# The embedding gates and the HGRN values as Strassen-type 2x2 block products, in a kernel for one Trainium2 core

## The chip, the core and the metric

The kernel runs on one core of a Trainium2 chip. A core has a matrix engine (TensorE, PE in the profile, with its weight loads as PEld), a vector engine (VectorE, DVE), an activation engine (ScalarE, ACT), GpSimd (POOL) and SyncE (SP), whose queue issues most of the loads; POOL issues the others. Each engine works through its own instructions in order and waits for others by semaphores. The metric is the time of one execution on the device in microseconds (us); lower is better.

## The reference, cut to what matters

512 tokens, width 1024, two layers. Layer 0 mixes tokens by multi-head latent attention, layer 1 by HGRN2, a gated linear recurrence.

```python
for i in range(2):
    h = mla_mixer(x, ...) if i == 0 else hgrn2_mixer(x, ...)
    x = layer_norm(alpha * x + h, ...)
    x = layer_norm(alpha * x + (silu(x @ w_g) * (x @ w_u)) @ ffn_w_down[i], ...)
    x = x + sigmoid(x @ ple_w_gate[i]) * (p[i] @ ple_w_proj[i])
# in hgrn2_mixer: proj = x @ w_in; q, f, v, gate are its four parts of 1024 columns
```

The change concerns three products of 512 x 1024 by 1024 x 1024: `x @ ple_w_gate[0]`, `x @ ple_w_gate[1]`, and the values `v` of the HGRN2 layer.

## The kernel before, in words

Tokens lie in four tiles of 128. Every float32 product is made of three matmuls on split operands: each operand is cut into a high part of fewer bits and a low part (the rest), and `mm3` adds high·high, high·low and low·high in PSUM. `split` makes both parts: ACT copies the source into the high part with rounding, DVE subtracts it from the source for the low part. `split_dma` does without DVE: ACT writes the high part, ACT writes its negative into the low part, and a DMA issued by POOL adds the source from memory onto that. `unit` loads a weight unit of 128 x 1024 by SP into one of 3 buffers `raw` and splits it into `whi` and `wlo` (5 buffers each).

The activations must be transposed to be left factors. A result of a stage that is needed so is put down by `defer`, and `flush` later lets PE transpose it (`to_feat`, four 128 x 128 transposes into a `tp` bank) and calls the sink that splits it. `Pair` is the plain sink: one split per half tile. `Winograd` serves the FFN's first product, `gate_up`, which already computes 2x2 block products with seven instead of eight multiplications: its sink makes the blocks A11 to A22 and four sums S1 to S4 from them, and `prep` makes the weight sums T1 to T4 for the next block while the present one is multiplied.

`rows` is the plain product: for each token tile and half of the columns 24 matmuls of 512 columns into one bank, then `consume`. `ple` runs `ple_w_proj` (8 banks of 6 matmuls), whose banks ACT copies into `pp`, and then `rows` for the gate with a sigmoid, a product and a sum per bank. In layer 0 the result goes through a `Pair` to `hgrn`, which begins with the values, again by `rows`; in layer 1 it goes out to memory, and the last bank there is cut in two of 256 columns (`cut`).

Each engine's order is fixed when the kernel is built: a scheduler places the instructions on the engines by the order of the program, the buffers' reuse and its own estimates. Buffers that matter here: 14 large slots (`big`), five buffers of 128 x 1024 under each of the tags `ma` and `mb`, and eight PSUM banks (`ps` three, `sc` two, `tp` two, `wg` one).

Of the kernel before, what the change touches and what calls it, by code (L numbers as in the profile page):

```python
# [20 lines left out]
F32 = mybir.dt.float32  # L21
F32R = mybir.dt.float32r
# [22 lines left out]
SM_SCALE = (NOPE + ROPE) ** -0.5  # L45
NLEV = 7
NEG = -1e30
T2 = 4
MID_BUFS = {"ma": 5, "mb": 5}
SLOTS = 14  # L50
# [24 lines left out]
class Rows:  # L75


    def __init__(self, b, dt=F32):
        self.z = [b.slot([P, 2, D], dt) for _ in range(NT // 2)]

    def __call__(self, t, cols=slice(None)):
        return self.z[t // 2][:, t % 2, cols]
# [14 lines left out]
        self.b.split(hi, lo, ps)  # L97


class Winograd:  # L100

    def __init__(self, b):
        self.b = b
        two = lambda: [b.slot([P, 2, 4, 256], F32R) for _ in range(2)]
        self.a1, self.s13, self.s24 = two(), two(), two()
        self.a2 = [b.slot([P, 2, 4, 256], F32R) for _ in range(2)]
        self.raw = [b.mid([P, 4, 256]) for _ in range(2)]  # L110
        self.at = {}

    def __call__(self, name):

        if name in ("A21", "A22"):
            z = self.a2[name == "A22"]
            return z[:, 0], z[:, 1]
        z, n = {"A11": (self.a1, 0), "A12": (self.a1, 1), "S1": (self.s13, 0), "S3": (self.s13, 1),
                "S2": (self.s24, 0), "S4": (self.s24, 1)}[name]
        return z[0][:, n], z[1][:, n]  # L120

    def sink(self, t, n, ps):
        b, nc = self.b, self.b.nc
        cs = slice(t % 2 * P, t % 2 * P + P)
        if t < 2:
            b.split(self.a1[0][:, n, :, cs], self.a1[1][:, n, :, cs], ps)
            nc.scalar.activation(self.raw[n][:, :, cs], ps, AF.Copy)
            return
        b.split(self.a2[n][:, 0, :, cs], self.a2[n][:, 1, :, cs], ps)
        if n == 0:  # L130
            a21 = b.small([P, 4, P], tag="t2", bufs=T2)
            nc.scalar.activation(a21, ps, AF.Copy)
            sx = b.mid([P, 2, 4, P], tag="mb")
            nc.vector.tensor_tensor(out=sx[:, 1], in0=self.raw[0][:, :, cs], in1=ps, op=ALU.subtract)
            self.at[t] = a21, sx
            return
        a21, sx = self.at.pop(t)
        sy = b.mid([P, 2, 4, P], tag="mb")
        nc.vector.tensor_tensor(out=sx[:, 0], in0=ps, in1=a21, op=ALU.add)
        nc.vector.tensor_tensor(out=sy[:, 0], in0=ps, in1=sx[:, 1], op=ALU.subtract)  # L140
        nc.vector.tensor_tensor(out=sy[:, 1], in0=self.raw[1][:, :, cs], in1=sy[:, 0], op=ALU.subtract)
        b.split(self.s13[0][:, :, :, cs], self.s13[1][:, :, :, cs], sx)
        b.split(self.s24[0][:, :, :, cs], self.s24[1][:, :, :, cs], sy)


class Builder:
# [201 lines left out]
        return self.small([P, 4], tag="lnst", bufs=6)  # L348


    def rows(self, lhs, units, consume, cut=()):

        for t in range(NT):
            n = 256 if t in cut else 512
            for c in range(0, 512, n):
# [8 lines left out]
                consume(t, slice(c, c + n), ps)  # L364

    def out_proj(self, lhs, src, x, ln):

        xT = Winograd(self)
        gb = self.ln_params(ln)
        st = [self.new_stats() for _ in range(NT)]  # L370
        self.rows(lhs, [self.unit(src[0, u]) for u in range(4)], lambda t, c, ps: self.ln_half(x, t, 0, ps, st[t]))
# [4 lines left out]
        self.rows(lhs, [self.unit(src[1, u], u % 2 == 0) for u in range(4)], fin)  # L376
        return xT


    def gate_up(self, l, xT):  # L380
# [3 lines left out]
        nc, v = self.nc, self.nc.vector  # L384
# [85 lines left out]
        for half in range(2):  # L470
            for j in range(2):
                plain(hs[j], ws[j], half)
                self.flush()
# [4 lines left out]
    def ffn(self, l, x, xT, ln):  # L478
        hT = self.gate_up(l, xT)
        gb = self.ln_params(ln, True)  # L480
        yT = Pair(self)
        acc = [(self.bank(f), self.bank(g)) for f, g in (("tp", "tp"), ("sc", "sc"), ("ps", "ps"), ("ps", "wg"))]
# [12 lines left out]
        for k in range(NF - NL):  # L495
            w, h = self.unit(self.i["ffn_w_down"][l, k]), hsplit(k)
            for t in range(NT):
                part(k, t, h, w)
        last = [(k, self.unit(self.i["ffn_w_down"][l, k]), hsplit(k)) for k in range(NF - NL, NF)]
        for t in range(NT):  # L500
            for k, w, h in last:
                part(k, t, h, w)
            self.flush()
            st = self.new_stats()
            for n in range(2):
                self.ln_half(x, t, n, acc[t][n], st)
            self.ln_finish(x, t, st, gb, yT.sink)
        return yT


    def ple(self, l, x, xT, last):
        nc = self.nc
        praw = self.mid([P, 2, S])
        nc.sync.dma_start(praw, self.i["p"][l])
        pT = (self.mid([P, 2, S], F32R), self.mid([P, 2, S], F32R))
        self.split(pT[0], pT[1], praw)
        pp = Rows(self)
        yT = None if last else Pair(self)
        for n in range(2):
            w = self.unit(self.i["ple_w_proj"][l, n])  # L520
            for t in range(NT):
                ps = self.bank()
                for k in range(2):
                    self.mm3(ps, [z[:, k, t * P:(t + 1) * P] for z in pT], [z[:, k * 512:(k + 1) * 512] for z in w], k == 0, k == 1)
                nc.scalar.activation(pp(t, slice(n * 512, (n + 1) * 512)), ps, AF.Copy)
        self.flush()
        for n in range(2):
            def fin(t, c, ps):
                sg = self.small([P, 512], tag="t2", bufs=T2)[:, c]
                c = slice(n * 512 + c.start, n * 512 + c.stop)  # L530
                nc.scalar.activation(sg, ps, AF.Sigmoid)
                xs = x(t, c)
                nc.vector.tensor_tensor(out=sg, in0=sg, in1=pp(t, c), op=ALU.mult)
                nc.vector.tensor_tensor(out=xs, in0=xs, in1=sg, op=ALU.add)
                if yT is None:
                    nc.sync.dma_start(self.out[:, t, c], xs)
                else:
                    self.defer(xs, yT.sink, t, n)
            self.rows(xT, [self.unit(self.i["ple_w_gate"][l, n, u]) for u in range(4)], fin, (NT - 1,) if last and n else ())
        return yT  # L540


# [196 lines left out]
    def hgrn(self, xT):  # L739
        nc = self.nc  # L740
        v_, a_ = nc.vector, nc.scalar
        i = self.i
# [6 lines left out]
        for n in range(2):  # L749
            def fin(t, c, ps):  # L750
                a_.activation(vv(t, slice(n * 512, (n + 1) * 512)), ps, AF.Copy)
            self.rows(xT, [self.unit(i["hgrn_w_v"][n, u]) for u in range(4)], fin)

        on = Rows(self)
        W2 = 4 * P
# [8 lines left out]
        for p in range(H // 2):  # L764
# [7 lines left out]
            for hh in range(2):  # L772
# [4 lines left out]
                for q in range(2):  # L777
                    w = self.unit(i["hgrn_w_fq"][h, q])
                    ps = self.bank()
                    for kc in range(KC):  # L780
                        self.mm3(ps, [z[:, kc * P:(kc + 1) * P] for z in w], xT(kc), kc == 0, kc == KC - 1)
# [192 lines left out]
```

## Time and profile before

| | before |
|---|---|
| median of 3 runs | 1299.7 us (1298.95 to 1300.2) |
| profiled execution | 1299.13 us, span 1297.0 us |
| PE busy | 1272.0 us (98%) |
| PE weight loads | 1134.2 us (87%) |
| DVE busy | 809.7 us (62%) |
| ACT busy | 658.5 us (51%) |
| POOL busy | 154.7 us (12%) |
| bytes read from memory | 153.05 MB |

Shares are of the span. The matmuls' busy time is modelled and overlaps, so how long a row of matmuls takes is read from their starts. "L200" is a line of the kernel; lines of helpers (L179, L180: `split`; L200 to L202: `mm3`) stand for all who call them, and the names of the tiles tell which call it is.

### The profile page before, as it was taken

To read this page: it belongs to the slowest core of one execution; us is meant where nothing else is said; L and a number is where in the kernel's file an instruction comes from. 1 tells how busy PE (TensorE), PEld (TensorE's weight loads), DVE (VectorE), ACT (ScalarE), POOL (GpSimd) and SP (SyncE) were. 2 spreads that over 40 slices of the span, in tenths; PEclk is the share of its full clock that TensorE was granted. 3 is DMA by queue.
4 is the path that set the end of the run, shared out by engine and by line. 5 is a ranking of instruction groups with operands and counts; after the bars stand their busy time and mean duration, and the time that the engine had idled before them with its cause. 6 is when DMAs were issued, how large, how long until landed. Compare 5 with 4: busy or idle time off the path is not lost.

```text
span 1297.0 us, 20093 instructions
## 1 busy us (share of the span) xinstructions
PE 1272.0 (98%) x7900; PEld 1134.2 (87%) x7900; DVE 809.7 (62%) x1452; ACT 658.5 (51%) x1140; POOL 154.7 (12%) x167
## 2 busy tenths in 40 slices
PE   8999999999999999999999999999999999999998
PEld 8788889999999888888888887888999999888887
DVE  7998488677675332943377776449777676433463
ACT  6666357767764222533334344327767765422352
POOL 0200041111110000100002220023111111000000
PEclk9999999999999999999999999999999999999999
DMA  7213027877884323232412120323888786323231
GB/s 228 68 63 131 26 89 180 210 181 175 186 187 136 98 98 114 85 109 65 133 62 66 66 78 21 115 80 86 213 205 186 181 186 164 119 97 98 94 98 49
DMA packets 47614, 156.45 MB, mean 121 GB/s; under 512 B 5664, under 2 KB 5920, under 8 KB 47264
## 3 DMA queue, kind: packets, MB, share of 16 engines
q1 hardware_dynamic: 36000, 123.71, 29.7%
q0 software_dynamic: 11520, 31.46, 14.0%
q8 instruction: 62, 1.02, 0.3%
q14 instruction: 32, 0.26, 0.1%
HBM read 153.05 MB, written 2.10 MB: 120 GB/s over the span
## 4 chain that ended last, share of the span: by engine, by line
PE 83%; DVE 7%; DMA 4%; ACT 3%; issue 2%; POOL 1%; SPq 0%; DVEq 0%; ACTq 0%; POOLq 0%
PE ps L200 18%; PE ps L201 18%; PE ps L202 18%; PE sc L200 3%; DMA raw<-ffn_w_in 3%; PE sc L201 3%; PE sc L202 3%; PE wg L201 2%; PE wg L200 2%; PE wg L202 2%; PE tp L304 2%; PE sc L812 2%; PE tp L201 2%; PE tp L202 2%; PE tp L200 2%
## 5 line engine op out<-in xcount | busy, mean ns | idle before, releaser
L180 DVE TENSOR_TENSOR wlo<-raw,whi 128x1024 fp32r<-128x1024 f32 (+1 forms) x123 | 148.4, 1209 | 206.2 <-ACT whi L179 204.5
L179 ACT ACTIVATE whi<-raw 128x1024 fp32r<-128x1024 f32 (+1 forms) x135 | 139.5, 1038 | 230.1 <-PE wg L202 125.7
L200 PE MATMUL ps<-big,whi 128*128 128x256 f32 (+1 forms) x768 | 236.9, 308 | 0.0
L202 PE MATMUL ps<-big,wlo 128*128 128x256 f32 (+1 forms) x768 | 236.7, 308 | 0.0
L201 PE MATMUL ps<-big,whi 128*128 128x256 f32 (+1 forms) x768 | 235.5, 307 | 0.0
L200 PE MATMUL ps<-whi,big 128*128 128x512 f32 (+2 forms) x440 | 170.6, 388 | 1.0 <-ACT big L179 1.0
L202 PE MATMUL ps<-whi,big 128*128 128x512 f32 (+2 forms) x440 | 168.2, 382 | 0.0
L201 PE MATMUL ps<-wlo,big 128*128 128x512 f32 (+2 forms) x440 | 168.0, 382 | 0.0
L201 PEld LDWEIGHTS ps<-big,whi 128*128 128x128 f32 x768 | 146.8, 191 | 5.4
L202 PEld LDWEIGHTS ps<-big,wlo 128*128 128x128 f32 x768 | 146.8, 191 | 5.2
L200 PEld LDWEIGHTS ps<-big,whi 128*128 128x128 f32 x768 | 146.9, 191 | 4.8
L200 PEld LDWEIGHTS ps<-whi,big 128*128 128x128 f32 x440 | 82.9, 188 | 15.4 <-ACT big L179 1.2
L202 PEld LDWEIGHTS ps<-whi,big 128*128 128x128 f32 x440 | 82.7, 188 | 15.6
L201 PEld LDWEIGHTS ps<-wlo,big 128*128 128x128 f32 x440 | 82.9, 188 | 14.4
L210 POOL TENSOR_TENSOR rr<-rv,mhalf 128x1 f32<-128x1 f32 (+2 forms) x28 | 26.6, 951 | 481.3 <-DVE rv L208 481.3
L180 DVE TENSOR_TENSOR wlo<-ma,whi 128x1024 fp32r<-128x1024 f32 x40 | 49.0, 1224 | 34.2 <-ACT whi L179 34.2
L202 PE MATMUL ps<-whi,ma 128*128 128x512 f32 x164 | 64.2, 392 | 0.0
L201 PE MATMUL ps<-wlo,ma 128*128 128x512 f32 x164 | 64.2, 392 | 0.0
L200 PE MATMUL ps<-whi,ma 128*128 128x512 f32 x164 | 64.0, 390 | 0.0
L186 POOL DMA_DIRECT2D ma<-ffn_w_in x40 | 34.8, 870 | 234.4 <-DVE big L460 150.8
L439 ACT ACTIVATE part<-ps 128x256 f32<-128x256 f32 x120 | 44.5, 374 | 25.3 <-PE ps L202 24.8
L180 DVE TENSOR_TENSOR mb<-ma,mb 128x1024 fp32r<-128x1024 f32 x40 | 48.9, 1222 | 6.3 <-ACT mb L179 3.4
(309 smaller groups left out, 3071.8 us busy)
## 6 DMA issues: line engine op xcount, KB each, us to landing
raw<-ffn_w_in SPq DMA_DIRECT2D x88, 512.0 KB, 4.6
raw<-ffn_w_down SPq DMA_DIRECT2D x44, 512.0 KB, 3.5
wlo<-ffn_w_in POOLq DMA_DIRECT2D x40, 512.0 KB, 7.3
ma<-ffn_w_in POOLq DMA_DIRECT2D x40, 256.0 KB, 7.0
raw<-ple_w_gate SPq DMA_DIRECT2D x16, 512.0 KB, 3.5
raw<-hgrn_w_fq SPq DMA_DIRECT2D x16, 512.0 KB, 3.5
raw<-mla_w_o SPq DMA_DIRECT2D x8, 512.0 KB, 3.6
raw<-hgrn_w_v SPq DMA_DIRECT2D x8, 512.0 KB, 4.4
```

Of the source, the lines that this page charges most:

```text
L179: self.nc.scalar.activation(hi, src, AF.Copy)
L180: (eng or self.nc.vector).tensor_tensor(out=lo, in0=src, in1=hi.bitcast(F32), op=ALU.subtract)
L186: self.nc.gpsimd.dma_start(lo, src, accum_op=ALU.add)
L200: mm(ps, a[0], b[0], start=start, stop=False, skip_group_check=more)
L201: mm(ps, a[0], b[1], start=False, stop=False, skip_group_check=more)
L202: mm(ps, a[1], b[0], start=False, stop=stop, skip_group_check=more)
L210: nc.gpsimd.tensor_tensor(out=r, in0=v, in1=self.mhalf[:, :n], op=ALU.pow)
L304: self.nc.tensor.transpose(out=ps[:, c * P:(c + 1) * P], in_=src[:, c * P:(c + 1) * P], identity=self.ident)
L439: copy = lambda dst, src: nc.scalar.activation(dst, src[:, :N], AF.Copy)
L812: nc.tensor.matmul(ps[:, c * P:(c + 1) * P], X[:, c * P:(c + 1) * P], pair_view(cs[0][:, :, 1, :], cs[1][:, :, 0, :]), start=True, stop=True)
```

## The change

Three pieces belong together.

First, `rows` gives way to a new function `square` for the three products. It cuts tokens (tiles 0, 1 against 2, 3), depth and columns in halves and makes seven products of 256 x 512 by 512 x 512, each 24 matmuls of 512 columns, where eight were. The weight sums T1 to T4 are made on DVE and split ("made"); three blocks are weights as they are, split by `split_dma` ("given"): SP loads each block as before, and B21 and B22 a second time for that. Partial sums are kept on ACT (128 x 512 copies) and joined with the last product by DVE in `consume`, ahead of the sigmoid.

Second, the left factors are made at the transposes for these products too: `Factors` replaces `Winograd` and, ahead of `square`, `Pair`.

Third, the token tiles go in the order 2, 3, 0, 1 in `out_proj` and `ffn`, `gate_up`'s plain units do half 1 first, `p` and its split lie in `mb` buffers, and the cut of the last bank is gone.

```diff
+ORDER = (2, 3, 0, 1)
-class Winograd:
+class Factors:
+    def __init__(self, b, whole=False, a21=True):
...
+        if whole:
+            for n in range(2):
+                w = [b.slot([P, 4, S], F32R) for _ in range(2)]
+                for m in range(2):
+                    self.z[f"A{m + 1}{n + 1}"] = [z[:, :, m * 256:(m + 1) * 256] for z in w]
+                self.z[n] = w
+            names = []
+        else:
+            names = ["A21", "A22", "A11", "A12"] if a21 else ["A22", "A11", "A12"]
+        for name in names + ["S1", "S2", "S3", "S4"]:
+            z = b.slot([P, 2, 4, 256], F32R)
+            self.z[name] = z[:, 0], z[:, 1]
...
+    def put(self, name, cs, src):
+        hi, lo = self.z[name]
+        self.b.split(hi[:, :, cs], lo[:, :, cs], src)
+
     def sink(self, t, n, ps):
+        v = self.b.nc.vector
         cs = slice(t % 2 * P, t % 2 * P + P)
+        name = f"A{2 if t >= 2 else 1}{n + 1}"
+        if name in self.z:
+            self.put(name, cs, ps)
+        if name == "A21":
+            if t == 2:
+                self.p, self.q = self.b.mid([P, 4, 256]), self.b.mid([P, 4, 256])
+            self.b.nc.scalar.activation(self.p[:, :, cs], ps, AF.Copy)
             return
+        p, q = self.p[:, :, cs], self.q[:, :, cs]
+        if name == "A22":
+            v.tensor_tensor(out=q, in0=ps, in1=p, op=ALU.add)
+            self.put("S1", cs, q)
+        elif name == "A11":
+            v.tensor_tensor(out=q, in0=q, in1=ps, op=ALU.subtract)
+            self.put("S2", cs, q)
+            v.tensor_tensor(out=p, in0=ps, in1=p, op=ALU.subtract)
+            self.put("S3", cs, p)
+        else:
+            v.tensor_tensor(out=q, in0=ps, in1=q, op=ALU.subtract)
+            self.put("S4", cs, q)
...
+    def square(self, xT, src, consume):
...
+        def given(z, i, j):
+            w = []
+            for u in range(2):
+                w.append((wt("whi"), wt("wlo")))
+                self.split_dma(*w[u], z[u], src_of(i, j, u))
+            return w
+        def made(z):
+            w = []
+            for u in range(2):
+                w.append((wt("whi"), wt("wlo")))
+                self.split(*w[u], z[u])
+            return w
+        def product(ps, s, w, more=False):
+            for t in range(2):
+                for kc in range(4):
+                    self.mm3(ps[t], [z[:, kc, t * P:(t + 1) * P] for z in s],
+                             [z[:, kc % 2 * 512:kc % 2 * 512 + 512] for z in w[kc // 2]],
+                             kc == 0 and not more, kc == 3, more)
+            self.flush()
...
+        for u in range(2):
+            r11.append(load(0, 0, u, raw))
+            r12.append(load(0, 1, u, ma))
+        r22 = [load(1, 1, u, ma) for u in range(2)]
+        t3, t1 = r22, r12
+        for u in range(2):
+            v.tensor_tensor(out=t3[u], in0=r22[u], in1=r12[u], op=ALU.subtract)
+            v.tensor_tensor(out=t1[u], in0=r12[u], in1=r11[u], op=ALU.subtract)
+        C = [self.bank(), self.bank("wg")]
+        product(C, xT("S1"), made(t1))
+        u1 = keep(C, "ma")
+        r21 = [load(1, 0, u, mb) for u in range(2)]
+        t2 = [mb() for _ in range(2)]
+        t4 = r21
+        comb(t2, t3, r11, ALU.add)
+        comb(t4, t2, r21, ALU.subtract)
+        d = [self.bank("sc"), self.bank("sc")]
+        product(d, xT("A22"), made(t4))
+        g1 = keep(d, "mb")
+        A = [self.bank(), self.bank()]
+        product(A, xT("A11"), given(r11, 0, 0))
+        g0 = keep(A, "mb")
+        product(A, xT("S2"), made(t2), True)
+        u0 = keep(A, "ma")
+        product(A, xT("S3"), made(t3), True)
+        for t in range(2):
+            consume(2 + t, 0, g1[:, t], A[t], ALU.subtract)
+            consume(2 + t, 1, u1[:, t], A[t], ALU.add)
+        B = [self.bank("sc"), self.bank("sc")]
+        product(B, xT("A12"), given([load(1, 0, u, raw) for u in range(2)], 1, 0))
+        for t in range(2):
+            consume(t, 0, g0[:, t], B[t], ALU.add)
+        product(C, xT("S4"), given([load(1, 1, u, raw) for u in range(2)], 1, 1), True)
+        for t in range(2):
+            consume(t, 1, u0[:, t], C[t], ALU.add)
...
     def ple(self, l, x, xT, last):
-        yT = None if last else Pair(self)
+        yT = None if last else Factors(self, whole=True)
...
+        def fin(t, n, s, ps, op):
+            nc.vector.tensor_tensor(out=sg, in0=ps, in1=s, op=op)
+            nc.scalar.activation(sg, sg, AF.Sigmoid)
...
+        self.square(xT, self.i["ple_w_gate"][l], fin)
...
+        def values(t, n, s, ps, op):
+            v_.tensor_tensor(out=vv(t, slice(n * 512, (n + 1) * 512)), in0=ps, in1=s, op=op)
+        self.square(xT, i["hgrn_w_v"], values)
```

In the whole program PE's rows go from 7349 to 7253, DVE's from 1372 to 1474, ACT's from 1036 to 1113, POOL's from 172 to 190.

Three places show how the orders moved. The first is ACT at the end of layer 0's FFN, where `ple_w_proj`'s banks are copied out. Before (L335 is LayerNorm's Square, L525 the copy of a bank, L179 the high part of a split):

```order
L335 ACTIVATE t_932_5796,lnst_5793<-big_1741,lnst_5793 128x1024
L525 ACTIVATE big_5861<-ps_5873 128x512
L525 ACTIVATE big_5861<-ps_5881 128x512
L525 ACTIVATE big_5862<-ps_5889 128x512
L525 ACTIVATE big_5862<-ps_5897 128x512
L179 ACTIVATE big_5015<-tp_5826 128x4x128
L179 ACTIVATE whi_5977<-raw_5975 128x1024
L179 ACTIVATE big_5017<-tp_5833 128x4x128
L335 ACTIVATE t_938_5843,lnst_5840<-big_1741,lnst_5840 128x1024
```

and now (L349 the Square, L626 the copy, L193 the high part):

```order
L193 ACTIVATE big_5018<-ma_5738 128x4x128
L193 ACTIVATE big_5015<-tp_5846 128x4x128
L193 ACTIVATE big_5019<-ma_5739 128x4x128
L349 ACTIVATE t_937_5859,lnst_5856<-big_1740,lnst_5856 128x1024
L626 ACTIVATE big_5877<-ps_5893 128x512
L626 ACTIVATE big_5877<-ps_5901 128x512
L626 ACTIVATE big_5878<-ps_5909 128x512
L193 ACTIVATE whi_6004<-ma_5988 128x1024
L626 ACTIVATE big_5878<-ps_5917 128x512
```

The first four copies stood ahead of the last tile's Square; now they stand behind it, and the fourth behind T1's high part as well.

The second place is DVE between the gate of layer 0 and the values. Before (L533 and L534 are the gate's product and sum, L180 a low part, of a transpose where it reads `tp`, of a weight where it writes `wlo`):

```order
L533 TENSOR_TENSOR t_1009_6246<-t_1009_6246,big_5862 128x512
L180 TENSOR_TENSOR big_5866<-tp_6239,big_5865 128x4x128
L534 TENSOR_TENSOR big_1741<-big_1741,t_1009_6246 128x512
L180 TENSOR_TENSOR wlo_6302<-raw_6299,whi_6301 128x1024
L180 TENSOR_TENSOR wlo_6308<-raw_6305,whi_6307 128x1024
L180 TENSOR_TENSOR wlo_6314<-raw_6311,whi_6313 128x1024
L533 TENSOR_TENSOR t_1012_6282<-t_1012_6282,big_5862 128x512
L180 TENSOR_TENSOR big_5866<-tp_6275,big_5865 128x4x128
```

and now (L632 joins the product with the kept part, L635 and L636 are product and sum, L194 a low part, L156 a sum of `Factors`, L436 and L437 make T3 and T1 of the values):

```order
L636 TENSOR_TENSOR big_1740<-big_1740,t_1037_6364 128x512
L632 TENSOR_TENSOR t_1038_6369<-wg_6003,ma_6157 128x512
L635 TENSOR_TENSOR t_1038_6369<-t_1038_6369,big_5877 128x512
L194 TENSOR_TENSOR big_5882<-tp_6431,big_5881 128x4x128
L636 TENSOR_TENSOR big_1740<-big_1740,t_1038_6369 128x512
L436 TENSOR_TENSOR ma_6389<-ma_6389,ma_6383 128x1024
L156 TENSOR_TENSOR ma_6260<-tp_6431,ma_6260 128x4x128
L437 TENSOR_TENSOR ma_6383<-ma_6383,raw_6381 128x1024
L436 TENSOR_TENSOR ma_6391<-ma_6391,ma_6387 128x1024
L194 TENSOR_TENSOR big_5886<-ma_6260,big_5886 128x4x128
L437 TENSOR_TENSOR ma_6387<-ma_6387,raw_6385 128x1024
L194 TENSOR_TENSOR wlo_6400<-ma_6383,whi_6399 128x1024
```

The first weight units of the values were split amid the gate's last tiles; now their sums and low parts (the last row is the first) stand behind the whole of the gate's `consume`.

The third place is ACT in the gate of layer 0, after the second product. Now (L424 keeps a bank, L193 is a high part, L198 and L199 the two passes of `split_dma`):

```order
L193 ACTIVATE whi_6055<-mb_6041 128x1024
L198 ACTIVATE whi_6088<-raw_5986 128x1024
L198 ACTIVATE whi_6093<-raw_5990 128x1024
L199 ACTIVATE wlo_6089<-whi_6088 128x1024
L424 ACTIVATE mb_6083<-sc_6049 128x512
L199 ACTIVATE wlo_6094<-whi_6093 128x1024
```

Before, ACT had only the sigmoids and the splits of the gate's next units there; now the given block B11 follows the last high part of T4.

More of the change, by code (lines that the diff above doesn't have):

```diff
@@ L348, in new_stats, with rows @@
         return self.small([P, 4], tag="lnst", bufs=6)
[L351 to L355, printed above, removed]
+    def rows(self, lhs, units, consume, order=range(NT)):
+        for t in order:
+            for c, n in ((0, 512),):
                 ps = self.bank()[:, :n]
@@ L366, in out_proj @@
     def out_proj(self, lhs, src, x, ln):
[L368 removed]
+        xT = Factors(self)
         gb = self.ln_params(ln)
         st = [self.new_stats() for _ in range(NT)]
[L371 removed]
+        self.rows(lhs, [self.unit(src[0, u]) for u in range(4)], lambda t, c, ps: self.ln_half(x, t, 0, ps, st[t]), ORDER)
         def fin(t, c, ps):
@@ L375, in fin @@
             self.ln_finish(x, t, st[t], gb, xT.sink)
-        self.rows(lhs, [self.unit(src[1, u], u % 2 == 0) for u in range(4)], fin)
+        self.rows(lhs, [self.unit(src[1, u], u % 2 == 0) for u in range(4)], fin, ORDER)
         return xT
@@ L469, in gate_up @@
         ws = [[self.unit(win[j, q], True) for q in range(2)] for j in range(2)]
-        for half in range(2):
+        for half in (1, 0):
             for j in range(2):
@@ L526, in ple @@
         self.flush()
[L527 to L539, printed above, removed]
+        def fin(t, n, s, ps, op):
+            c = slice(n * 512, (n + 1) * 512)
+            sg = self.small([P, 512], tag="t2", bufs=T2)
+            nc.vector.tensor_tensor(out=sg, in0=ps, in1=s, op=op)
+            nc.scalar.activation(sg, sg, AF.Sigmoid)
+            xs = x(t, c)
+            nc.vector.tensor_tensor(out=sg, in0=sg, in1=pp(t, c), op=ALU.mult)
+            nc.vector.tensor_tensor(out=xs, in0=xs, in1=sg, op=ALU.add)
+            if last:
+                nc.sync.dma_start(self.out[:, t, c], xs)
+            else:
+                self.defer(xs, yT.sink, t, n)
+        self.square(xT, self.i["ple_w_gate"][l], fin)
         return yT
```

76 lines of the change are left out of this document (33 added, 43 removed).

## The prediction, made before the changed kernel was run

> **What bounds the kernel now.** I read the page's busy times first, then PE's waits, then a table by stage for the places the change touches.
>
> ```profile
> span 1297.0 us, 20093 instructions
> PE 1272.0 (98%) x7900; PEld 1134.2 (87%) x7900; DVE 809.7 (62%) x1452; ACT 658.5 (51%) x1140; POOL 154.7 (12%) x167
> ...
> PE tp L200 <- ACT whi L179: 5.2, 1, 5.2
> PE tp L304 <- DVE big L344: 4.7, 4, 1.3
> PE ps L200 <- ACT part L439: 3.0, 5, 1.0
> ...
> 518.00:550.00 32.00, 32.00 (x156) 26.11 (x155) 28.17 (x57) 19.59 (x31) 4.82 (x5) 1.00 0.26 81
> 550.00:595.00 45.00, 45.00 (x212) 37.20 (x211) 21.93 (x30) 16.07 (x22) 0.00 (x0) 1.00 0.26 85
> 595.00:642.00 47.00, 47.00 (x212) 38.94 (x211) 13.28 (x13) 15.59 (x20) 0.00 (x0) 1.00 0.33 103
> ...
> 1250.00:1297.00 47.00, 42.70 (x211) 36.12 (x210) 16.98 (x24) 9.94 (x15) 0.00 (x0) 0.98 0.19 68
> ```
>
> TensorE (PE) is busy 98% of the span, and its three largest waits come to 13 us, 5.2 of them the first load. The window rows give, after the length, busy PE, weight load, DVE, ACT and POOL, then granted clock, DMA share and GB/s: the end of the FFN with `ple_w_proj` (518 to 550), the gate of layer 0 (550 to 595), the HGRN values (595 to 642), the gate of layer 1 (from 1250). PE never waits in the first three. So matmuls taken out count in full, and so does every wait put in. The first row warns: ahead of the gate DVE is already busy 28.17 of 32 us. The profiled execution took 1299.13 us, 2.1 beyond its span; the median of the runs is 0.6 us above it.
>
> **Matmuls removed.** Durations, from the timelines of PE, DVE and ACT (start, duration):
>
> ```profile
> 550.23 0.39 PE L202 MATMUL ps<-whi,big 128*128 128x512 f32 x1
> ...
> 555.67 0.39 PE L202 MATMUL ps<-whi,big 128*128 128x512 f32 x1
> ...
> 594.59 0.39 PE L202 MATMUL ps<-whi,big 128*128 128x512 f32 x1
> ...
> 595.17 0.47 PE L200 MATMUL ps<-whi,big 128*128 128x512 f32 x1
> ...
> 542.77 0.69 DVE L180 TENSOR_TENSOR big<-tp,big 128x512 fp32r<-128x512 f32 x1
> 543.37 0.14 DVE L334 TENSOR_SCALAR lnst<-lnst 128x1 f32<-128x1 f32 x1
> 543.43 1.22 DVE L180 TENSOR_TENSOR wlo<-raw,whi 128x1024 fp32r<-128x1024 f32 x1
> 544.56 0.68 DVE L180 TENSOR_TENSOR big<-tp,big 128x512 fp32r<-128x512 f32 x1
> ...
> 548.18 1.05 ACT L179 ACTIVATE whi<-raw 128x1024 fp32r<-128x1024 f32 x1
> 549.13 1.08 ACT L179 ACTIVATE big<-tp 128x512 fp32r<-128x512 f32 x2
> ```
>
> Between the first two PE rows lie 24 matmuls: 5.44 us, 0.227 each. Before, a 1024 x 1024 product over four token tiles takes eight banks of 24 matmuls (eight chunks, three passes of `mm3`); a square takes seven products of 24 (two tiles, four chunks, three passes). So each square, 168 instead of 192, saves 5.44 us; three save 16.3. That is the whole gain. The last gate matmul of layer 0 starts at 594.59, the first of the values at 595.17. DVE starts to start is 0.60 us at 128x512 (542.77 to 543.37) and 1.13 at 128x1024 (543.43 to 544.56); ACT 0.95 at 128x1024 (548.18 to 549.13), about 0.55 at 128x512.
>
> **What is added, and why little of it hides.** A square wants DVE to make T1 to T4 (8 of 128x1024) and their low halves (8 more): 16 x 1.13 = 18 us, where `unit` had 8 low halves, 9 us. ACT gets 8 keeps and 6 more passes, POOL 6 accumulate DMAs. PE needs T1 first and T4 second, at the moment when DVE still works off LayerNorm and transposes. I laid the changed instruction order out by hand, engine by engine, with these durations, in the clock of before.
>
> *Start of the gate.* After the FFN's last matmul (first row below) ACT holds the copies of `ple_w_proj`'s banks (L626) behind the Square of the last tile; that Square waits for DVE's L348, which now stands behind eight sink operations and a T combination whose load could start only when the FFN's last matmuls freed an `ma` buffer.
>
> ```profile
> 535.43 0.40 PE L202 MATMUL wg<-whi,ma 128*128 128x512 f32 x1
> ...
> 539.96 0.60 ACT L525 ACTIVATE big<-ps 128x512 f32<-128x512 f32 x1 [0.76 <-PE ps L202]
> ...
> 543.91 1.14 ACT L335 ACTIVATE t<-big,lnst 128x1024 bf16<-128x1024 f32 x1
> ...
> raw<-ple_w_gate SPq DMA_DIRECT2D x16, 512.0 KB, 3.5
> ```
>
> In before, four copies (the third is the second row here) go ahead of that Square (third row). With three `ps` banks the fourth `ple_w_proj` product, which PE could start at 540.7 (535.7, three products of 6 x 0.227 and two sets of transposes), now waits for a copy. The load lands at 535.7 + 3.5 = 539.2 at the earliest; DVE's sinks, held by the transposes before, and its L348 take until 546, the Square 1.3, the copy 0.6: 548.1, 7.4 us lost. Then `r22[1]`'s load on SP waits for T1's first low half on DVE (about 552.9); by 3.5 us of landing (the last row above) the second T1 starts on DVE at 556.7, takes two passes of 1.13 and ACT's hi (560.4, PE waits 2.7), and its low half stands behind seven sink operations (7 x 0.60): 564.5 to 565, another 3.2. Together 13.3 us, and T4, whose own combinations and low halves stand behind these (four more passes of 1.13 and a hi), is done at about 573.6 instead of 560.2. Bounds: 0, if all this hid under PE as in before, and 18 us, if nothing of DVE's 16 passes did; I keep the count.
>
> *B11 behind a DMA.* A "given" block's low half is made by ACT (L199) and an accumulate DMA on POOL (L200), not by DVE. ACT reaches it only after T4's last hi (about 570), so POOL issues at 573.
>
> ```profile
> wlo<-ffn_w_in POOLq DMA_DIRECT2D x40, 512.0 KB, 7.3
> ma<-ffn_w_in POOLq DMA_DIRECT2D x40, 256.0 KB, 7.0
> ...
> DMA to landing us min/median/max: 5.5/7.3/8.3
> ```
>
> 7.3 us from issue to landing (third row: the 40 of 512 KB) gives 580.6 against 573.6: 7.0 us of idle PE, 5 to 8 by the row's ends. In before's FFN the same DMAs are issued a block ahead and hidden; here nothing lies between T4 and A11. Half the bytes take 7.0 (second row), so I don't expect a quieter queue to help. Against this stands the Trainium skill, "DMA: Bandwidth & Descriptors", section "Anatomy of one DMA — SWDGE (gpsimd) path": 2.0 us plus bytes at 436 GB/s, an estimate of 3.2 us here; the trace disagrees, and by it the sum would be some 12 us smaller over the three squares. B21 and B22 go the same way; S2 and S3, 10.9 us of matmul, cover most, and I count 1 us each.
>
> So layer 0's gate ends at 594.9 (the last matmul's start and length) - 5.4 + 13.3 + 7.0 + 2 = 611.8: +17.
>
> *From the gate to the values.* This is the largest term. From S3's end (about 597) to the low halves of the values' T1, DVE's queue holds 46 operations of 128x512 (consume, and the factors of `Factors(whole=True)`: six splits' low halves, S1 to S4) and 6 of 128x1024: 46 x 0.60 + 6 x 1.13 = 34.4, so 632. PE has only A12·B21, S4·B22 and transposes to do, until 611.8. In before the values begin 0.6 us after the gate's last matmul starts, since `Pair` wants 8 low halves there. Net loss 632 - 611.8 - 0.6 = 19.6; below, 13 us if a third of these operations runs ahead of S3's end; above 24, as two of the loads wait for buffers that DVE frees in this very stretch. T4 of the values then waits 2.5 (four passes of 1.13 against 2.7 us of half a product), B11's DMA 5.5. The values: 19.6 + 2.5 + 5.5 - 5.4 = +22; with layer 0's gate +39 by their end.
>
> *Gate of layer 1.* Same start (13.3 + 7.0 + 2 - 5.4 = +17). The tail:
>
> ```profile
> 1292.42 0.28 PE L202 MATMUL ps<-whi,big 128*128 128x256 f32 x1
> ...
> 1293.62 0.42 DVE L534 TENSOR_TENSOR big<-big,t 128x256 f32<-128x256 f32 x1
> ...
> out<-big SPq DMA_DIRECT2D x7, 256.0 KB, 2.0
> ```
>
> Before, 4.6 us from the last matmul to the end of the span, with 256 columns. After, with 512: add 0.68, sigmoid 0.60, two of 0.68, then the 256 KB to land: 2.64 + about 3.4 (the 1293.62 row's distance to the end, with its own length) = 6; +1.5. The 48 cut matmuls (0.12 apart) cost what 24 whole ones do, nothing more.
>
> *The rest at nothing.* The order 2, 3, 0, 1, plain half 1 first, the Factors made at out_proj's transposes (8 DVE operations for 9 of other shapes) and `praw` from `mb`: under PE's 32 us in windows like the first; if the cover goes, 1 us each at two places.
>
> Sum: -16.3 + 2 x 22.3 + 27.6 + 1.5 = +57.4, and -1 for out_proj: 1299.1 + 56 = 1355 (the median like it).
>
> **Rivals.**
>
> *Only the backlogs bite* (the gates' starts hide): ACT's and DVE's places in the queue are as I say, but the LayerNorm tail may leave them time, as PE's last FFN rows overlap them. Then 2 x 13.3 and the 1 us terms go: 1355 - 30 = 1325. For it: DVE 28.17 of 32 busy leaves 4 us per gate; against: the copy's place behind the Square is fixed by the order.
>
> *The other side: DVE keeps ahead of PE.* One mechanism: DVE and ACT finish each square's blocks before PE asks, since the loads come early (DMA share 0.26 to 0.33) and ACT is half idle (16 of 45 us). Then only the gain and the tail are left: 1299.1 - 16.3 + 1.5 = 1284. It decides where the waits of all three squares together fall under 15 us; I count 72, so it needs four fifths of them to go.
>
> *PE comes back slow after the waits.*
>
> ```profile
> 5.84 0.44 PE L200 MATMUL sc<-whi,big 128*128 128x288 f32 x1
> 6.08 0.51 PE L201 MATMUL tp<-wlo,big 128*128 128x288 f32 x1
> ...
> 8.07 0.44 PE L202 MATMUL sc<-whi,big 128*128 128x288 f32 x1
> 8.31 0.37 PE L200 MATMUL ps<-whi,big 128*128 128x288 f32 x1
> 8.52 0.29 PE L201 MATMUL ps<-wlo,big 128*128 128x288 f32 x1
> 8.65 0.29 PE L202 MATMUL ps<-whi,big 128*128 128x288 f32 x1
> ```
>
> After 5.2 us with nothing to do, PE ran the first 3.1 us at 0.24 us a matmul and then at 0.13, though the granted clock reads 1.00: 13 matmuls x 0.11 = 1.4 us lost. After every one of my waits over 5 us (two per gate, two at the values) that could come again: 6 x 1.4 = 8.4, of which the half ahead of another wait is hidden: +4 to +8, 1359 to 1363. Against it: no later wait of before is longer than 1.3 us, so none shows where it starts. The Trainium skill, "TensorE: Matmul & The Clock Gate", Part 1, has the same thing as a rule: half rate after an idle window of about 3.4 us, and full rate after as much work; the first rows agree with it.
>
> **How the numbers follow.** Waits as counted, 0.45 (1340 to 1372); with slow restarts, 0.2; only the backlogs, 0.25 (1315 to 1335); the other side, 0.07; balance within 0.2% (2.6 us, about what a measurement of this kernel can tell from no change), 0.03. The time is the first case's, 1355. The range 1316 to 1380 takes in the unknown costs at both ends (DMA landing ±5, the boundary 13 to 24, the starts 0 to 18) and leaves out the other side and little more. Faster 0.07, same 0.03, slower 0.90.
>
> **What would show it.** PE's waits should list about 7 us on ACT's L626 copy (`ps L214`), 3 and 3 on T1's hi and low half, 7 on POOL's L200 with `ple_w_gate`, and one of 15 to 20 on DVE's `wlo` before the values. PE's busy time falls by some 16, its share to under 94%. DVE should be busy nearly throughout 597 to 632. Wrong would be a gate whose first product starts within 2 us of 549, or values that follow the gate at once.

## The result, and the profile after

The changed kernel takes 1385.1 us (median, 1384.3 to 1388.2) against 1299.7: 1.066 times, 95% interval 1.064 to 1.068. It is slower, as forecast, but by 85 us where 55 were forecast, and 5 us beyond the range.

The page of the changed kernel (busy times; then PE's busy tenths and the granted clock in 40 slices):

```profile
span 1382.5 us, 20147 instructions
PE 1288.3 (93%) x7804; PEld 1137.6 (82%) x7804; DVE 884.1 (64%) x1550; ACT 714.7 (52%) x1217; POOL 169.8 (12%) x185
...
PE   8999989999999997694899999998999999999777
...
PEclk9999999999999999886999999999999999999988
```

PE's busy time rose by 16 us, where a fall of 16 was forecast, though 96 of its instructions went. The two last rows show why: at the holes in PE's work the granted clock falls too, and matmuls there count as busy for longer. PE's waits (what waited, for what: us in total, times, the longest):

```profile
PE ps L215 <- DMA wlo<-ple_w_gate: 16.3, 3, 9.1
PE ps L214 <- ACT big L626: 15.6, 2, 7.8
PE tp L318 <- DVE big L636: 11.3, 3, 6.6
PE tp L318 <- DVE big L358: 9.7, 4, 3.5
PE ps L215 <- DVE wlo L194: 6.5, 3, 2.4
```

The stages, by the starts of PE's matmuls in the two traces (us; the end by the span):

| event | before | after | lag | lag added | forecast |
|---|---|---|---|---|---|
| last FFN matmul, layer 0 | 535.4 | 539.6 | 4.1 | +4.1 | -0.5 |
| last gate matmul, layer 0 | 594.6 | 623.5 | 28.9 | +24.8 | +17 |
| first matmul after the values | 639.3 | 696.6 | 57.3 | +28.4 | +22 |
| last FFN matmul, layer 1 | 1235.7 | 1297.4 | 61.6 | +4.3 | -0.5 |
| end | 1297.0 | 1382.5 | 85.5 | +23.9 | +18.3 |

Slices of layer 0's gate and its passage to the values (length, then busy PE, weight load, DVE, ACT, POOL, granted clock, DMA share, GB/s):

```profile
544.00:552.00 8.00, 1.26 (x9) 0.81 (x8) 7.83 (x15) 3.49 (x6) 0.00 (x0) 0.81 0.00 1
...
584.00:592.00 8.00, 3.66 (x9) 2.87 (x10) 0.67 (x1) 0.00 (x0) 0.00 (x0) 0.50 0.75 182
...
624.00:632.00 8.00, 0.96 (x8) 0.52 (x5) 7.88 (x14) 4.30 (x8) 0.00 (x0) 0.72 0.04 15
632.00:640.00 8.00, 2.17 (x8) 1.43 (x8) 7.30 (x12) 2.62 (x5) 0.00 (x0) 0.50 0.39 131
```

Three holes of three kinds: in the first DVE is full and PE stands; in the second nobody computes until PE starts again at 588.34, and the DMA engines are at 0.75; in the third DVE is full again, before the values.

### The profile page after: what moved, and what is told of

Its sections match the earlier page's. It is cut to its first block, busy times and chain, and to the rows that moved or that the text cites. A ratio compares the mean times of both kernels' runs of the same rounds, so it can differ in the third digit from the quotient of the medians.

```text
span 1382.5 us, 20147 instructions
## 1 busy us (share of the span) xinstructions
PE 1288.3 (93%) x7804; PEld 1137.6 (82%) x7804; DVE 884.1 (64%) x1550; ACT 714.7 (52%) x1217; POOL 169.8 (12%) x185
## 4 chain that ended last, share of the span: by engine, by line
PE 42%; DVE 4%; DMA 3%; issue 3%; ACT 1%; POOL 0%; DVEq 0%; POOLq 0%; ACTq 0%; SPq 0%
PE ps L215 9%; PE ps L216 9%; PE ps L214 9%; PE sc L914 1%; PE sc L215 1%; PE sc L216 1%; PE sc L214 1%; PE wg L215 1%; PE wg L216 1%; PE wg L214 1%; DMA wlo<-hgrn_w_v 1%; DMA raw<-ffn_w_in 1%; DMA wlo<-ple_w_gate 1%; PE tp L318 1%; PE tp L214 1%
## 5 line engine op out<-in xcount | busy, mean ns | idle before, releaser
L193 ACT ACTIVATE whi<-raw 128x1024 fp32r<-128x1024 f32 (+1 forms) x111 | 114.2, 1032 | 236.5 <-PE wg L216 137.2
L194 DVE TENSOR_TENSOR wlo<-raw,whi 128x1024 fp32r<-128x1024 f32 (+1 forms) x99 | 119.0, 1205 | 177.3 <-ACT whi L193 176.6
L215 PE MATMUL ps<-wlo,big 128*128 128x512 f32 (+1 forms) x336 | 133.2, 397 | 25.7 <-DMA wlo<-ple_w_gate 16.3
L214 PE MATMUL ps<-whi,big 128*128 128x512 f32 (+1 forms) x336 | 134.1, 400 | 3.3 <-ACT whi L193 2.8
L216 PE MATMUL ps<-whi,big 128*128 128x512 f32 (+1 forms) x336 | 132.1, 393 | 0.0
L194 DVE TENSOR_TENSOR wlo<-ma,whi 128x1024 fp32r<-128x1024 f32 x52 | 63.6, 1222 | 58.3 <-ACT whi L193 58.3
L215 PEld LDWEIGHTS ps<-wlo,big 128*128 128x128 f32 x336 | 65.3, 194 | 41.7 <-DMA wlo<-ple_w_gate 18.1
L214 PEld LDWEIGHTS ps<-whi,big 128*128 128x128 f32 x336 | 64.7, 193 | 16.7 <-ACT whi L193 4.3
L216 PEld LDWEIGHTS ps<-whi,big 128*128 128x128 f32 x336 | 65.0, 194 | 12.4
L198 ACT ACTIVATE whi<-raw 128x1024 fp32r<-128x1024 f32 x58 | 60.9, 1055 | 9.7 <-DMA raw<-ffn_w_in 5.1
L199 ACT ACTIVATE wlo<-whi 128x1024 fp32r<-128x1024 f32 x58 | 60.8, 1048 | 0.4
L539 ACT ACTIVATE part<-ps 128x256 f32<-128x256 f32 x120 | 44.3, 373 | 24.4 <-PE ps L216 24.1
L193 ACT ACTIVATE whi<-ma 128x1024 fp32r<-128x1024 f32 x52 | 54.6, 1051 | 4.1 <-DVE ma L437 2.3
L214 PE MATMUL ps<-whi,ma 128*128 128x512 f32 x132 | 51.5, 391 | 0.0
```

The lines of the kernel that those rows point to most:

```text
L193: self.nc.scalar.activation(hi, src, AF.Copy)
L194: (eng or self.nc.vector).tensor_tensor(out=lo, in0=src, in1=hi.bitcast(F32), op=ALU.subtract)
L198: self.nc.scalar.activation(hi, raw, AF.Copy)
L199: self.nc.scalar.activation(lo, hi.bitcast(F32), AF.Copy, scale=-1.0)
L214: mm(ps, a[0], b[0], start=start, stop=False, skip_group_check=more)
L215: mm(ps, a[0], b[1], start=False, stop=False, skip_group_check=more)
```

## The experiments

All times are medians; "after" is the changed kernel, 1385.1.

**POOL's weight splits beside LayerNorm.** The first lag, 4.1 us, comes ahead of any square. DVE, POOL and PE of the changed kernel at the end of layer 0's `out_proj` (start, duration; in brackets the idle time before it and what ended that):

```profile
184.22 5.58 DVE L358 SCALAR_TENSOR_TENSOR big<-big,rr,ma 128x512 f32<-128x512 f32 x2
...
184.01 5.24 POOL L194 TENSOR_TENSOR wlo<-raw,whi 128x1024 fp32r<-128x1024 f32 x2
...
187.30 1.09 PE L318 MATMUL tp<-ident,big 128*128 128x128 f32 x4 [3.52 <-DVE big L358]
```

```diff
-        self.rows(lhs, [self.unit(src[1, u], u % 2 == 0) for u in range(4)], fin, ORDER)
+        self.rows(lhs, [self.unit(src[1, u]) for u in range(4)], fin, ORDER)
-        ws = [[self.unit(win[j, q], True) for q in range(2)] for j in range(2)]
+        ws = [[self.unit(win[j, q]) for q in range(2)] for j in range(2)]
```

> The changed kernel, but the weight splits that POOL makes at the end of out_proj and the start of gate_up (2 + 4 units in each layer) are made by DVE. In the trace of the changed kernel a DVE operation of LayerNorm at 184.22 lasts 5.58 us for two, while POOL runs two such splits (184.01, 5.24 us), and PE then waits 3.52 us for it; the first ple_w_proj matmul comes 4.1 us later than before in layer 0, and 4.3 more in layer 1. Theory (POOL's split holds DVE up): both places give most of that back, -6 to -8 us: 1377 to 1379. Rival (DVE simply has too much to do there): six more passes of 1.13 us per place on DVE, so 0 to +10 us: 1385 to 1395.

1375.0 us, 10.1 below after. The same two operations of DVE, without POOL's splits:

```profile
182.36 1.41 DVE L358 SCALAR_TENSOR_TENSOR big<-big,rr,ma 128x512 f32<-128x512 f32 x2
```

5.58 became 1.41 us, and the last FFN matmul of layer 0 starts at 535.6, as in before. Then the other parts of the change alone (Factors at out_proj, tile order, half 1 first, p in `mb`, no cut), with plain products:

> The kernel before with the change's other parts alone: Factors at out_proj's transposes, tiles in the order 2, 3, 0, 1, gate_up's plain units half 1 first, p in mb buffers, no cut bank; the three products stay plain. Theory (the 4.1 + 4.3 us ahead of the gates belong to these parts): 1308 to 1311, the lost cut of the last bank included. Rival (they cost nothing, as the prediction had it, and come only with the squares): 1299 to 1302.

1308.3 us (ratio 1.0068, 1.0053 to 1.0083): 8.7 above before, as the stages said. With POOL's splits on DVE in this kernel too, and in before:

> The change's other parts with plain products, and the weight splits of out_proj and gate_up made by DVE instead of POOL. With POOL's splits this kernel stood 8.6 us above before. Theory (those 8.6 us are POOL's splits holding up DVE's LayerNorm, in the new order of the tiles): all comes back, 1299 to 1302, the lost cut of the last bank (1 to 2 us) included. Rival (Factors' sinks and the order cost part of it themselves): 1303 to 1308.

> The kernel before, with the same splits made by DVE instead of POOL. In its own trace a pair of LayerNorm's DVE operations lasts 3.55 us instead of 1.41 beside POOL's splits (180.33, POOL 180.91 for 7.59), and PE's waits there come to 4.7 us in four. Theory (the two engines hold each other up there as well): -1 to -4 us, 1296 to 1299. Rival (before's order leaves room, and six more passes per layer on DVE cost what is won): 1299 to 1303.

1299.7 (1.0003, 0.9994 to 1.0012) and 1299.7 (1.0001, 0.9992 to 1.0010). So the whole 8.7 us is POOL holding DVE up, and in the new order only: in before taking the splits off POOL gains nothing. The order of the tiles and the Factors' sinks at out_proj cost nothing by themselves. DVE was stretched in before too, at the same place (DVE, then POOL, then DVE again):

```profile
180.33 3.55 DVE L344 SCALAR_TENSOR_TENSOR big<-big,rr,ma 128x512 f32<-128x512 f32 x2
...
180.91 7.59 POOL L180 TENSOR_TENSOR wlo<-raw,whi 128x1024 fp32r<-128x1024 f32 x3 [0.75 <-ACT whi L179]
...
183.80 0.67 DVE L327 SCALAR_TENSOR_TENSOR big<-big,ps 128x512 f32<-128x512 f32 x1
```

There PE waited 1.03 us for it, in the changed kernel 3.52.

**The slow clock.** After the first hole PE comes back at half rate:

```profile
553.11 0.79 PE L214 MATMUL ps<-whi,mb 128*128 128x512 f32 x1 [7.82 <-ACT big L626]
553.71 0.63 PE L215 MATMUL ps<-wlo,mb 128*128 128x512 f32 x1
554.13 0.63 PE L216 MATMUL ps<-whi,mb 128*128 128x512 f32 x1
...
559.23 0.40 PE L216 MATMUL ps<-whi,mb 128*128 128x512 f32 x1
559.46 0.39 PE L214 MATMUL ps<-whi,mb 128*128 128x512 f32 x1
```

0.427 us from start to start instead of 0.227, for 13 matmuls. To see what this costs, matmuls of no use were put where PE waits (`busy(a, b, n)`: n matmuls of 128x512 into a `tp` bank that nobody reads).

```diff
+                if n == 0 and t == 3:
+                    self.busy(pT[0][:, 0, 0:P], pT[0][:, 1, :], 30)
...
+        self.busy(w4[1][0][:, 0:P], w4[1][0][:, 512:1024], idle[0])   # ahead of A11 B11
...
+        self.busy(w5[1][0][:, 0:P], w5[1][0][:, 512:1024], idle[1])   # behind S4 B22
...
+        self.square(xT, self.i["ple_w_gate"][l], fin, (34, 0 if last else 25))
...
+        self.square(xT, i["hgrn_w_v"], values, (12, 0))
```

> The changed kernel, with matmuls of no use (results thrown away) put on PE ahead of its long waits: 30 ahead of the fourth ple_w_proj product and 34 ahead of A11 B11 in both gates, 25 between gate and values, 12 ahead of A11 B11 in the values. 0.227 us each, they are shorter than the waits they stand in (7.8, 9.1, 10 and 6 us). Theory (the clock falls after idle time, and matmuls at 0.43 instead of 0.227 us cost 7.7 + 5.4 + 7.9 = 21 us in the three squares): most comes back, -12 to -20 us: 1365 to 1373, with the waits in the same places. Rival (what PE loses slow is hidden behind its next wait, since DVE, ACT and DMA set the pace): 1381 to 1389.

1384.7 us: nothing. The half-rate matmuls of 128x512 (rows of 0.63 us) in layer 0's gate and the values fell from 50 to 27, in layer 1's gate from 31 to 11, and the waits moved. PE of this kernel:

```profile
547.47 7.06 PE L329 MATMUL tp<-mb 128*128 128x512 f32 x30 [2.04 <-DVE lnst L354]
...
569.12 0.50 PE L214 MATMUL ps<-whi,big 128*128 128x512 f32 x1 [4.14 <-ACT whi L193]
```

The 30 matmuls keep PE at full rate; it finishes `ple_w_proj` early and waits 4.14 us for T1. The time is the rival's: 43 half-rate matmuls are gone, 8.6 us at 0.20 each, and nothing came of it. But this run doesn't show that a full clock is worth nothing, for the edit changed more than the clock. It moved DVE's order: the second sum for T1 starts at 566.7 behind the late tiles' sinks, in the changed kernel at 562.4 ahead of them, and that is where the 4.14 us come from. The matmuls also wait for a `tp` bank themselves (2.04 in the first row) and end 1.3 us after the wait that they should fill.

**The given blocks' DMA.** POOL's issue and PE's waits in the changed kernel's timeline, and then the landing times of all DMAs that POOL issues into `wlo`:

```profile
578.50 0.87 POOL L200 DMA_DIRECT2D wlo<-ple_w_gate  x1 [23.65 <-ACT wlo L199]
...
588.34 0.79 PE L215 MATMUL ps<-wlo,big 128*128 128x512 f32 x1 [9.08 <-DMA wlo<-ple_w_gate]
...
610.55 0.80 PE L215 MATMUL sc<-wlo,big 128*128 128x512 f32 x1 [2.15 <-DMA wlo<-ple_w_gate]
```

```profile
DMA to landing us min/median/max: 5.3/7.1/11.3
```

```diff
-                self.split_dma(*w[u], z[u], src_of(i, j, u))
+                self.split(*w[u], z[u])
```

> The changed kernel, but the given blocks B11, B21, B22 get their low halves from DVE (128x1024, 1.13 us each, six per square) instead of ACT's second pass and POOL's accumulate DMA. Theory (the DMA is the wait): the waits on wlo's DMA in the changed kernel's trace (16.3 + 2.2 in the gates, 3.1 + 2.8 in the values, 24.4 us) go, and with them the slow matmuls behind them that no later wait hides (2 to 3 us per square); DVE is busy only 0.7 to 3.3 of 8 us in the slices from 576 to 608, so it has room: -20 to -30 us, 1355 to 1365. Rival (DVE is the bound there too): 18 more passes come to 20 us, the waits move to DVE's low halves, and the time is 1378 to 1392.

1356.3 us: 28.8 below after, by far the largest single edit that leaves the products alone. DVE had the room. In the changed kernel's timeline PE's waits on these DMAs come to 24.3 us in the three squares; the half-rate matmuls fell from 81 to 49, so some of the slow work behind those waits came back with them. Both edits together:

> The two edits together: given blocks split on DVE, and out_proj's and gate_up's weight splits on DVE too, so POOL makes neither splits nor accumulate DMAs around the squares. Theory (the two costs lie in different stages): the gains add, 10 us below the kernel with the first edit alone. Rival (DVE is full): less than 5 us below it.

1345.2: 11.2 more. These two costs are separate.

**The copies behind the Square.**

```diff
-                ps = self.bank()
+                ps = self.bank(("ps", "ps", "ps", "sc", "sc", "wg", "ps", "ps")[n * NT + t])
```

> The changed kernel, but the eight ple_w_proj products take the banks ps ps ps sc sc wg ps ps instead of three ps in turn, so the fourth needs no copy by ACT. Its wait of 7.8 us (ACT L626) is gone. Theory (DVE's queue sets when T1 is ready, whatever PE does before): PE comes to T1 earlier and waits longer there, the time stays within 4 us of 1385: 1381 to 1389. Rival (each wait counts by itself, as the sum of the prediction took them): -2 x 7.8, and the slow matmuls behind them, 1364 to 1370.

1378.7: 6.5 below after, between the two. PE's waits in this kernel:

```profile
PE ps L215 <- DMA wlo<-ple_w_gate: 16.5, 4, 7.3
...
PE ps L214 <- ACT big L626: 9.9, 2, 4.9
PE ps L215 <- DVE wlo L194: 7.4, 3, 2.8
```

The wait for the copies went from 15.6 to 9.9 us: it now stands at the seventh product, the first that needs a bank again. The 5.7 us that went did count, somewhat more than one for one, against the theory; the waits for T1's low halves rose by 0.9 only.

**The values.** Plain rows for them, no sums S1 to S4:

> The changed kernel, but the HGRN values are plain rows of 24 matmuls again and no sums S1 to S4 are made for them; both gates stay squares. By the stages of the two traces the values cost 28.4 us more than before. Theory (the stages add up, and the values' T1 behind DVE's queue is theirs): 1385 - 28 = 1357. Rival (the DVE backlog after the gate is the gate's own, consume and splits, and stays): -8 to -14 us, 1371 to 1377.

1351.2: 33.9 below after, more than the stage's 28.4; the rest lies in layer 0's gate, which no longer makes the sums (its and the values' lag together is 19.1 instead of 53.2), while layer 1's gate adds 24.1 as it did. DVE and PE of the changed kernel between gate and values:

```profile
617.47 0.68 DVE L194 TENSOR_TENSOR big<-tp,big 128x512 fp32r<-128x512 f32 x1
...
642.85 1.22 DVE L194 TENSOR_TENSOR wlo<-ma,whi 128x1024 fp32r<-128x1024 f32 x1
...
634.15 1.09 PE L318 MATMUL tp<-ident,big 128*128 128x128 f32 x4 [6.56 <-DVE big L636]
...
644.12 0.80 PE L215 MATMUL ps<-wlo,big 128*128 128x512 f32 x1 [1.70 <-DVE wlo L194]
```

From the first row to the second, the first low half of T1, DVE hardly stops, and PE waits for it in transposes and then in T1: 15.8 us in five waits. Whether the amount of DVE's work sets this was tried by leaving 16 of its operations out (and with them ten of ACT's: eight high parts and two copies):

```diff
-        yT = None if last else Factors(self, whole=True)
+        yT = None if last else Factors(self, whole=True, sums=False)
...
+        stand = {"S1": "A21", "S2": "A11", "S3": "A11", "S4": "A12"}
-        self.square(xT, i["hgrn_w_v"], values)
+        self.square(lambda k: xT(stand.get(k, k)), i["hgrn_w_v"], values)
```

> The changed kernel, with the sums S1 to S4 for the values left out (A21, A11, A11, A12 stand in for them, so the values are not the reference's): the same matmuls, weights and joins, but 16 fewer operations of 128x512 on DVE between the gate of layer 0 and the values, 9.6 us at 0.60. Theory (DVE's queue between the joins and T1 is the wait there): T1 comes 7 to 10 us earlier, 1375 to 1378, with layer 1 unchanged. Rival (the loads of the values' weights, which wait for ma buffers, or the joins' own wait for PE set it): 1382 to 1387.

1372.3: 12.8 below after, for 9.6 us of DVE work. Theory, and more: from the start of the gate's last matmul to the first one on T1's low half it is 11.0 us instead of 20.6, the 9.6 us exactly. The other 3 lie in the gate, whose order the edit moved as well (B11's wait is 5.8 instead of 9.1).

**Another order of the products.** The given blocks first, made like any unit while the FFN ends, T1 to T4 behind them, squares for the gates only. This kernel is built on before, with its tile order and its out_proj, and makes its factors in another order too:

```diff
+        A = [self.bank(), self.bank()]
+        product(A, xT("A11"), w11)
+        g0 = keep(A, "ma")
+        B = [self.bank("sc"), self.bank("sc")]
+        product(B, xT("A12"), w21)
...
+        comb(t3, r22, r12, ALU.subtract)
+        comb(t1, r12, r11, ALU.subtract)
+        C = [self.bank(), self.bank("wg")]
+        product(C, xT("S1"), made(t1))
```

> Squares for the two gates alone, in another order: tiles 0, 1, 2, 3 and the out_proj of before; the first two products are A11 B11 and A12 B21, whose weights are loaded and split like any unit while the FFN ends, then S1 T1, S2 T2, A22 T4, S4 B22, S3 T3, with T1 to T4 made while the first products run; all splits on DVE; the values plain. Saves 48 matmuls of 512 columns, 10.9 us. Theory (the loss is in the order: PE asks first for what is made last): waits of a few us are left per gate and the time comes to 1288 to 1303. Rival (the loss is in the amount of DVE's work around the gate, 16 passes and nine operations per late tile): each gate stays 10 us or more behind, 1315 to 1330.

1313.9 (1.0107, 1.0092 to 1.0122), nearly the rival's. And with the banks as above:

> The kernel of the two gates with the given blocks first, and the ple_w_proj products in the banks ps ps ps sc sc wg ps ps, so that none of the first six needs a copy by ACT. In that kernel's trace PE waits 3.3 us for such a copy in layer 0 and runs 13 matmuls at half rate after it (2.6 us). Theory (here PE's next products need nothing new from DVE for two products, so the wait counts): -4 to -10 us, 1304 to 1310. Rival (DVE, busy without a break from 536 to 557, sets T1 anyway): 1311 to 1316.

1309.1 (1.0072, 1.0058 to 1.0086). In this kernel's second gate the listed waits of PE from 1230 us on are

```profile
PE ps L244 <- ACT big L644: 6.1, 1, 6.1
PE ps L245 <- DVE wlo L224: 0.3, 1, 0.3
```

and the slice in which the first of them lies is

```profile
1248.00:1256.00 8.00, 1.95 (x6) 1.30 (x6) 8.00 (x14) 5.35 (x12) 2.73 (x1) 0.74 0.00 0
```

One wait is left, for a copy that ACT makes behind the last Square, while DVE is full (8.00 of 8). Last, the changed kernel with four edits at once (no splits on POOL in out_proj and gate_up, given blocks split on DVE, plain values, six banks):

> The changed kernel with four edits together: no splits on POOL in out_proj and gate_up, given blocks split on DVE, values plain, ple_w_proj in six banks. Singly they gave 10.1, 28.8, 33.9 and 6.5 us below 1385. Theory (they lie in different places, but for the values' share of the given blocks, about 8 of 28.8): 1385 - 10 - 21 - 34 - 6 = 1314, that is still 14 us above before though it has 48 matmuls fewer; what stays is DVE at the start of the two gates and the consume at their end. Rival (the waits shift into one another): 1325 or more.

1320.1, between the two: with two gates in the change's order the kernel is 20.5 us slower than before; with the given blocks first and the same banks, 9.5. The two kernels differ in the order of the tiles and in out_proj as well, so the share of the products' order alone is not shown. No version with a `square` beat before.

## Why the prediction was right in sign and wrong in size

- *The gain.* 5.44 us per square stands: it is counted in every stage above. It was never in doubt.
- *Start of the gate: right in sum, in part by luck.* From the last FFN matmul: the fourth `ple_w_proj` product forecast at 548.1 - 535.4 = 12.7, measured 553.1 - 539.6 = 13.5. T4's last matmul was forecast to end 38.2 after it, and ended at 39.5. But the waits there were 10.5 us and not 13.3 (none for T1's second high part, 2.4 for its low half), and slow matmuls filled the gap. Three more banks took 2.9 us of the 7.8 away per gate and gave 3.2: this wait counted as it was taken.
- *B11 behind a DMA: right in sum, by luck.* The step took 23.5 us for all three squares (7.0 + 7.0 + 5.5 and 1 each for B21 and B22 in the gates); PE's waits on these DMAs came to 24.3. Its parts were off both ways. B11 cost 9.1 and 4.7 in the gates and 2.4 in the values; B21 and B22, nearly free in the sum, cost 8.1. The 9.1 came where two DMAs are issued 1.6 us apart with loads beside them: the first was needed for 9.8 us (578.50 to 588.34), above the 8.3 at most of the row, which is the FFN's, where such DMAs of 512 KB are issued some 10 us apart. The 3.2 us, an estimate worked out from the Trainium skill, "DMA: Bandwidth & Descriptors", section "Anatomy of one DMA — SWDGE (gpsimd) path", was further off than the row.
- *From the gate to the values: right.* PE lost 20.0 us there (623.5 to 644.1, less the 0.6 of before) where 19.6 were forecast, and that the chain is DVE's the run without sums shows. DVE itself took longer, 40 us from the first join (L632, 604.1) to 644.1 instead of 34.4, since it waited 6 in between, mostly for PE; but the gate ended later as well. The lower bound doesn't follow: a third of 34.4 us is 11.5, which leaves 8 us and not 13.
- *"The rest at nothing": the step that failed outright.* The cover was there by count (8 operations for 9), but LayerNorm's operations there stood beside POOL's splits. The forecast was -1, the measured cost +8.7 alone, 8.4 by the two lags ahead of the gates, and 10.1 within the changed kernel. Before's rows at 180.33 and 180.91 show it; the prediction doesn't have them. The Trainium skill, "SBUF — State Buffer", section "SBUF: two separate sides", states it: DVE with two SBUF inputs and a GpSimd instruction that reads SBUF take turns on one port pair, and the loser blocks. The trace agrees: L358 reads two SBUF tiles and lasted 5.58 us beside 5.24 of POOL.
- *Waits at their own length alone: the other step that failed.* The first case's sum has no term for slow work after a wait; the rival that has one priced it at 1.4 us in six places, 4 to 8 us in all. The three squares hold nine such stretches with 81 rows of 0.63 us, 16 us at 0.20 each; the first alone is 13 x 0.20 = 2.6, since the matmuls here have 512 columns.
- *The other rivals.* "Only the backlogs bite" was wrong: both kinds bit. DVE did not keep ahead of PE either.

Where the 29 us between forecast and result lie can be counted by PE's starts. Ahead of the two gates: 8.4 instead of -1, shown by runs to be POOL and DVE. In the three squares: 63 us of waits, 9 less than the 72 counted, and 28 us by which PE's own work ran longer than before's, where the sum has none. Sixteen of the 28 are the half-rate matmuls; the rest (the first matmul after each wait, transposes, gaps) wasn't taken apart. The tail: 2.3 instead of 1.5. This tells where the time went, not what a full clock would give back. Where another engine sets the next wait, PE merely arrives earlier, and the run that filled the waits gained nothing; but it moved DVE's order too, so this share stays open.

## What to carry to other kernels

This kernel, at 98% on one engine, had no slack on it to hide new waits: 16 us of matmuls were bought with work on queues that were already full at that very place. Ask of every added operand not how much work it is but when it can be ready, and try first the products whose operands are ready anyway: the kernel in that order lost 9.5 us with its two gates instead of 20.5, though it differs in more than that. Price a wait with the slow matmuls behind it, and ask whether another wait will swallow them. And look beside each engine that a step leans on for another that stretches it, at the very rows in the trace of before, before costing the step at nothing.

## What the runs showed of the hardware

- POOL's splits stretched DVE several-fold: 1.41 us became 5.58 for two operations with both inputs in SBUF, while in before L327, which reads one input from PSUM, kept its 0.67 amid POOL's 7.59. POOL's own splits took 2.39 to 2.79 us each.
- A PE that has waited can run at half rate, for 3 to 6 us (13 starts 0.427 apart from 553.11 on). It did so after as little as 2.15 us of waiting (the row at 610.55 lasts 0.80, and the next six start 0.43 apart), while after a wait of 2.42 us at 570.20 the starts were 0.23 apart: the length of the wait alone doesn't decide. Nor does it always begin with the wait's end: after 2.59 us of waiting, at 1370.23, PE went on for 1.6 us before the starts were 0.43 apart. In the Trainium skill, "TensorE: Matmul & The Clock Gate", Part 1, the idle window is about 3.4 us and runs freely; the waits of 2.15 and 2.59 us are shorter than that, so here less than a whole idle window was enough.
- An accumulate DMA of 512 KB took 5.3 to 11.3 us to land in one kernel.
